# Hybrid retention and differential attention layer on one core: first transfers regrouped, first scores of four heads one slice later, last half block multiplied with normalized tokens

## The chip, the cores and the metric

The kernel runs on one core of a Trainium2 chip. The metric is the device time of one execution in microseconds (us), given as the median of several runs; a second source is one profiled execution, from which all rows below come. Engines are named as in the profile: PE (TensorE, matmuls), PEld (its weight loads, which overlap PE), DVE (VectorE), ACT (ScalarE), POOL (GpSimd) and SP (the queue that issues most transfers).

## What is computed

One encoder layer on 512 tokens of width 2048. Everything is float32 outside; inside, each matmul operand is split into a high and a low part, and a product is three matmuls.

```python
u = rmsnorm(h, attn_norm)
rq, rk, rv, rg, dq, dk, dv, dg = split(u @ w_in)
ro = retention(rope(rq), rope(rk) * RET_DK ** -0.5, rv)
ro = rmsnorm(ro, ret_gn) * silu(rg)
do = diff_attention(rmsnorm(dq, diff_qn), rmsnorm(dk, diff_kn), dv, lam)
do = rmsnorm(do, diff_subln) * (1.0 - lam_init) * silu(dg)
h = h + concatenate([ro, do]) @ w_out
gate = sigmoid(rmsnorm(h, ple_norm) @ w_ple_gate)
h = h + gate * (p @ w_ple_proj)
```

## The kernel before

Tokens lie along the free axis, features along the 128 partitions, so x is 16 tiles of 128 x 512. Each weight matrix is read once in pieces of 256 columns. `split` (L134 to L141) makes the high part on ACT (Copy, L137, or with a gain L140) and the low part on DVE (source minus high part, L138 or L141). `mm3` (L143 to L146) issues the three matmuls of a product.

**The start.** SP issues the first half of x's first tile, ACT's queue issues the first 256 columns of the dv weights and then `cols`, a small tile `ct` with all gains; SP goes on with the second half of x, the dq weights and the other tiles (L94 to L106). Six matmuls on a constant tile (`warm`) run meanwhile. The first product block needs the split of x, with its gain from `ct`, and the split of the dv weights.

**Slices.** After the start the program is a list of projections. A projection yields after each slice, twelve 512-column matmuls. `after(n, step)` puts a step into the agenda n slices ahead, and `tick` calls what is due. So attention steps stand between slices of matmuls of other projections, by tables written by hand: `QK` for the norms of q and k, `SCORES` and `TURNS` for the two heads of a pair and four blocks of 128 queries, `VALUES` for the products with v. A scheduler then orders each engine's instructions, mainly in the order in which the program writes them, and weight splits go ahead by a priority.

**Scores.** For one head and block, `scores` (L473 to L496) takes two PSUM banks from the tag `sc`, which has two. Each gets two matmuls (L484 with `k`, L485 with `kz`); DVE then writes a mask (MEMSET, L486) and takes the row maximum (TENSOR_REDUCE, L487); ACT takes the exponential out of the bank (L488) and reads the row sum. With that the bank is free. The next head's `scores` takes the same two banks. `stack_k` (L458 to L468) makes `k0`, `k1` and the low parts `kz` of a head from its normed `t_k`: two copies on ACT (L462, L463), and on DVE CAST, `kz`, CAST, `kz` (L464 to L467). There are four pairs of heads, numbered 0 to 3 here; in pairs 1 and 3 the scores stand between slices of a wide dv projection, in pairs 0 and 2 between slices of gate and q projections, where `silus` (L424 to L433) also switches ACT's function table.

**The gate stage.** After the output projection each residual tile `h_sb[b]` is split with its gain (`h_hi`, `h_lo`), unnormalized; the row factor `R1` (1/rms of each token) is multiplied in after the gate product. `output` (L834 to L842) does for one block: times R1 (DVE, L838), Sigmoid (ACT, L839), times the p projection (DVE, L840), plus h (DVE, L841), transfer out (SP, L842). The last projection has its weights in tiles of their own, and its second block of 128 features is done in two halves of 256 tokens, so that the chain behind the last matmul is short (L862 to L872).

Of the kernel before, what the change touches and what calls it, by code (L numbers as in the profile page):

```python
# [12 lines left out]
F32 = mybir.dt.float32  # L13
F32R = mybir.dt.float32r
AF = mybir.ActivationFunctionType
ALU = mybir.AluOpType
AX = mybir.AxisListType

P = 128
S = 512  # L20
D = 2048
KB = D // P
EPS = 1e-6
CW = 256
# [3 lines left out]
AHEAD = 600  # L28
WARM = 6
FIRST = ((0, 1), (1, 1)) + tuple((k, 2) for k in range(2, KB, 2))  # L30
SCORES = ((7, 11, 15, 19), (9, 13, 17, 21))
TURNS = ((10, 14, 18, 22), (12, 16, 20, 25))
VALUES = (25, 29)
QK = (4, 6)
# [4 lines left out]
def f(ap):  # L39
    return ap.bitcast(F32)  # L40
# [3 lines left out]
def tile_layer(  # L44
# [5 lines left out]
    w_out: bass.AP,  # L50
    w_gate: bass.AP,
    w_proj: bass.AP,
    cols: bass.AP,
    lams: bass.AP,
    cosT: bass.AP,
    sinT: bass.AP,
# [9 lines left out]
    nc = tc.nc  # L66
    PSUM = bass.MemoryType.PSUM

    const = ctx.enter_context(tc.tile_pool(name="const", bufs=1))
    upool = ctx.enter_context(tc.tile_pool(name="upool", bufs=1))  # L70
    wpool = ctx.enter_context(tc.tile_pool(name="wpool", bufs=4))
    vpool = ctx.enter_context(tc.tile_pool(name="vpool", bufs=1))
    onp = ctx.enter_context(tc.tile_pool(name="onp", bufs=1))
    tmp = ctx.enter_context(tc.tile_pool(name="tmp", bufs=2))
# [3 lines left out]
    def bank(tag, bufs, name):  # L78
# [5 lines left out]
    xt = [xp.tile([P, S], F32, tag=f"xt{k}", name=f"xt{k}") for k in range(KB)]  # L84
    raws = [[xp.tile([P, n, CW], F32, tag=f"raw{i}_{k}", name=f"raw{i}_{k}") for i in range(2)]
            for k, n in FIRST]
    ct = const.tile([P, 43], F32, name="ct")

    def load_w(q, b, i):
        k, n = FIRST[b]  # L90
        off = (OFF_DV, OFF_DQ)[i]
        q.dma_start(raws[b][i], w_in[k * P:(k + n) * P, off:off + CW].rearrange("(kb p) n -> p kb n", p=P))

    H = S // 2  # L94
    with tc.high_priority(offset=2 * AHEAD):
        nc.sync.dma_start(xt[0][:, :H], xT[0:P, :H])
        load_w(nc.scalar, 0, 0)
        nc.scalar.dma_start(ct, cols)
        nc.sync.dma_start(xt[0][:, H:], xT[0:P, H:])
        load_w(nc.sync, 0, 1)  # L100
        for b, (k, n) in enumerate(FIRST[1:], 1):
            for i in range(n):
                nc.sync.dma_start(xt[k + i], xT[(k + i) * P:(k + i + 1) * P, :])
                if i == 0:
                    load_w(nc.sync, b, 0)
                    load_w(nc.sync, b, 1)  # L106
# [16 lines left out]
    g_attn, g_ple, g_ret = ct[:, 0:16], ct[:, 16:32], ct[:, 32:40]  # L123
# [10 lines left out]
    def split(hi, lo, src, gain=None):  # L134

        if gain is None:
            nc.scalar.activation(hi, src, AF.Copy)  # L137
            nc.vector.tensor_tensor(lo, src, f(hi), ALU.subtract)  # L138
        else:
            nc.scalar.activation(hi, src, AF.Copy, scale=gain)  # L140
            nc.vector.scalar_tensor_tensor(lo, src, gain, f(hi), ALU.mult, ALU.subtract)  # L141

    def mm3(out, ah, al, bh, bl, start, stop):  # L143
        nc.tensor.matmul(out, lhsT=ah, rhs=bh, start=start, stop=False, skip_group_check=True)  # L144
        nc.tensor.matmul(out, lhsT=ah, rhs=bl, start=False, stop=False, skip_group_check=True)  # L145
        nc.tensor.matmul(out, lhsT=al, rhs=bh, start=False, stop=stop, skip_group_check=True)  # L146
# [62 lines left out]
    def after(n, *todo):  # L209
        agenda[clock[0] + n].extend(todo)  # L210
# [57 lines left out]
    R1 = const.tile([P, S], F32, name="R1")  # L268
# [89 lines left out]
    with start:  # L358
        ssum = xp.tile([P, S], F32, name="ssum")

        first = [[bank(*tag, f"acc_{name}0_{j}") for j in range(2)]
                 for tag, name in ((("acc", 4), "dv"), (("sc", 2), "dq"))]
        for b, (k0, n) in enumerate(FIRST):
            wh, wl = ([wpool.tile([P, 2, CW], F32R, tag=tag, name=f"{tag}{i}_{k0}") for i in range(2)]
                      for tag in ("whi", "wlo"))
            for k in range(k0, k0 + n):
                uh = upool.tile([P, S], F32R, tag=f"uh{k}", name=f"uh{k}")
                ul = upool.tile([P, S], F32R, tag=f"ul{k}", name=f"ul{k}")  # L370
                u_hi.append(uh)
                u_lo.append(ul)
                s = k - k0

                def split_w(i):
                    split(wh[i][:, s, :], wl[i][:, s, :], raws[b][i][:, s, :])

                if k == 0:
                    split_w(0)
                    split(uh[:, :H], ul[:, :H], xt[0][:, :H], g_attn[:, 0:1])  # L380
                    split(uh[:, H:], ul[:, H:], xt[0][:, H:], g_attn[:, 0:1])
                    split_w(1)
                else:
                    split(uh, ul, xt[k], g_attn[:, k:k + 1])
                    split_w(0)
                    split_w(1)
                v_products(first[0], k, wh[0][:, s, :], wl[0][:, s, :])
                fm_products(first[1], k, KB, wh[1][:, s, :], wl[1][:, s, :], u_hi, u_lo)
                sq = ssum if k == 0 else tmp.tile([P, S], F32, tag="sq", name=f"xsq{k}")
                nc.scalar.activation(sq, xt[k], AF.Square)  # L390
                if k:
                    nc.vector.tensor_tensor(ssum, ssum, sq, ALU.add)
        row_norm(ssum)

# [45 lines left out]
    with ExitStack() as st:  # L440
# [88 lines left out]
        def pair_jobs(hp):  # L529
# [26 lines left out]
            def queue_heads():  # L556
# [4 lines left out]
                for j, (s, t, v, n) in enumerate((diff_steps(2 * hp + j, pair) for j in range(2))):  # L561
                    for b in range(4):
                        after(late + SCORES[j][b], partial(s, b))
                        after(late + TURNS[j][b], partial(t, b))
# [193 lines left out]
    mixp = ctx.enter_context(tc.tile_pool(name="mixp", bufs=1))  # L758
# [20 lines left out]
    h_hi, h_lo, h_sb = [], [], []  # L779
    ssum = mixp.tile([P, S], F32, name="ssum2")  # L780
# [50 lines left out]
                fm_products(pp, k, 2, wh[:, k, :], wl[:, k, :], p_hi, p_lo)  # L831
        return pp

    def output(b, ag, pp, c):  # L834

        n = c.stop - c.start
        g = tmp.tile([P, S], F32, tag="t0", name=f"fg{b}_{c.start}")[:, :n]
        nc.vector.tensor_tensor(g, ag, R1[:, c], ALU.mult)  # L838
        nc.scalar.activation(g, g, AF.Sigmoid)  # L839
        nc.vector.tensor_tensor(g, pp[:, c], g, ALU.mult)  # L840
        nc.vector.tensor_tensor(h_sb[b][:, c], h_sb[b][:, c], g, ALU.add)  # L841
        nc.sync.dma_start(outT[b * P:(b + 1) * P, c], h_sb[b][:, c])  # L842

    def outputs(n, ag):
        pp = ple(n)
        for j in range(2):
            output(2 * n + j, ag[j], pp[j], slice(0, S))

    for n in range(7):
        run(proj_fm(w_gate, n * CW, KB, h_hi, h_lo, f"pg{n}", partial(outputs, n)))  # L850

# [2 lines left out]
    pp = ple(7, (("tp", 1), ("o", 1)))  # L854
    wv = w_gate.rearrange("(kb p) n -> p kb n", p=P)
    with tc.high_priority(offset=AHEAD):
        last = []
        for k0 in range(0, KB, 4):
            raw = wpool.tile([P, 4, CW], F32, tag="wraw", name=f"wr_pg7_{k0}", bufs=2)
            nc.sync.dma_start(raw, wv[:, k0:k0 + 4, 7 * CW:8 * CW])  # L860
            for s in range(0, 4, 2):
                wh, wl = (mixp.tile([P, 2, CW], F32R, tag=f"{t}{(k0 + s) // 2}", name=f"{t}_pg7_{k0 + s}")  # L862
                          for t in ("mh", "ml"))
                split(wh, wl, raw[:, s:s + 2, :])
                last.extend((wh[:, i, :], wl[:, i, :]) for i in range(2))
    for b, c in ((14, slice(0, S)), (15, slice(0, S // 2)), (15, slice(S // 2, S))):
        n = c.stop - c.start
        w = slice((b - 14) * P, (b - 13) * P)
        ag = bank("acc", 4, f"acc_pg7_{b}_{c.start}")[:, :n]
        for k, (wh, wl) in enumerate(last):  # L870
            mm3(ag, wh[:, w], wl[:, w], h_hi[k][:, c], h_lo[k][:, c], k == 0, k == KB - 1)
        output(b, ag, pp[b - 14], c)  # L872


def _tables():
# [49 lines left out]
```

## Time and profile before

| what | value |
|---|---|
| device time, median of 3 runs | 1083.37 us (1083.04 to 1083.54) |
| the profiled execution, device time | 1083.01 us |
| its span, first to last instruction | 1081.2 us |
| PE busy | 1074.7 us, 99% of the span |
| DVE busy | 652.9 us, 60% |
| ACT busy | 561.2 us, 52% |
| HBM read and written | 106.06 MB and 4.19 MB |

The span is 1.8 us shorter than the device time of the same execution. A busy PE is work plus pipelining: matmuls overlap, so a 512-column matmul that shows 0.39 us starts 0.23 us after the one before it, and a 256-column one with 0.28 us starts 0.12 us after.

### The profile page before, as it was taken

How to read it: one execution, taken by the hardware profiler on the slowest of the kernel's cores; microseconds unless marked ns; L12 is line 12 of the kernel's file. 1: busy time of each engine (PE TensorE's matmuls, PEld its weight loads, DVE VectorE, ACT ScalarE, POOL GpSimd, SP SyncE). 2: the span in 40 equal slices, each digit the busy share in tenths (PEclk: the TensorE clock that was granted, in tenths of full speed). 3: DMA queues.
4: the chain of work that ended last, by engine and by line, in shares of the span. 5: the costliest groups of instructions: out<-in, count | busy, mean ns of one | idle time of the engine just before them, and what ended most of it. 6: DMA issues, size and time to landing. Idle time of an engine off the chain costs nothing.

```text
span 1081.2 us, 13724 instructions
## 1 busy us (share of the span) xinstructions
PE 1074.7 (99%) x5090; PEld 900.7 (83%) x5090; DVE 652.9 (60%) x1211; ACT 561.2 (52%) x1044; POOL 4.9 (0%) x14
## 2 busy tenths in 40 slices
PE   9999999999999999999999999999999999999998
PEld 8888888888888888888888988888888888888887
DVE  8677658775968786577446866844334453334442
ACT  8477657565767755664436655743333343222330
POOL 0000000000000000000000000000000000000000
PEclk9999999999999999999999999999999999999999
DMA  9232322322232232243322332463333323333341
GB/s 318 62 95 80 96 79 79 96 81 78 79 98 72 66 98 79 79 136 92 102 87 91 97 100 75 155 200 96 97 98 98 98 88 121 124 117 114 120 136 40
DMA packets 100579, 111.15 MB, mean 103 GB/s; under 512 B 4384, under 2 KB 88992, under 8 KB 100512
## 3 DMA queue, kind: packets, MB, share of 16 engines
q1 hardware_dynamic: 97632, 105.40, 31.7%
q10 hardware_dynamic: 2880, 4.87, 1.3%
q8 instruction: 40, 0.66, 0.3%
q14 instruction: 27, 0.22, 0.1%
HBM read 106.06 MB, written 4.19 MB: 102 GB/s over the span
## 4 chain that ended last, share of the span: by engine, by line
PE 98%; DVE 1%; ACT 0%; DMA 0%; issue 0%; ACTq 0%
PE acc_pg L145 5%; PE acc_pg L144 5%; PE acc_pg L146 5%; PE acc_o L146 5%; PE acc_o L145 5%; PE acc_o L144 5%; PE acc_dv L144 3%; PE acc_dv L145 3%; PE acc_dv L146 3%; PE acc_dq L144 3%; PE acc_rg L144 3%; PE acc_dq L145 3%; PE acc_dg L144 3%; PE acc_dk L144 3%; PE acc_dg L146 3%; PE acc_dg L145 3%
## 5 line engine op out<-in xcount | busy, mean ns | idle before, releaser
L144 PE MATMUL acc_o<-mh,wh_o 128*128 128x512 f32 x256 | 99.6, 389 | 0.0
L145 PE MATMUL acc_o<-ml,wh_o 128*128 128x512 f32 x256 | 99.6, 389 | 0.0
L146 PE MATMUL acc_o<-mh,wl_o 128*128 128x512 f32 x256 | 99.6, 389 | 0.0
L137 ACT ACTIVATE wh_o<-wr_o 128x512 fp32r<-128x512 f32 x64 | 40.4, 631 | 113.4 <-PE acc_o L145 106.7
L138 DVE TENSOR_TENSOR wl_o<-wr_o,wh_o 128x512 fp32r<-128x512 f32 x64 | 44.2, 691 | 89.2 <-ACT wh_o L137 89.2
L137 ACT ACTIVATE wh_pg<-wr_pg 128x512 fp32r<-128x512 f32 x56 | 35.4, 632 | 102.1 <-PE acc_pg L145 88.5
L144 PE MATMUL acc_pg<-hh,wh_pg 128*128 128x512 f32 x224 | 87.1, 389 | 0.0
L145 PE MATMUL acc_pg<-hl,wh_pg 128*128 128x512 f32 x224 | 87.1, 389 | 0.0
L146 PE MATMUL acc_pg<-hh,wl_pg 128*128 128x512 f32 x224 | 87.1, 389 | 0.0
L138 DVE TENSOR_TENSOR wl_pg<-wr_pg,wh_pg 128x512 fp32r<-128x512 f32 x56 | 38.7, 690 | 69.4 <-ACT wh_pg L137 69.4
L145 PEld LDWEIGHTS acc_o<-ml,wh_o 128*128 128x128 f32 x256 | 48.1, 188 | 10.0
L144 PEld LDWEIGHTS acc_o<-mh,wh_o 128*128 128x128 f32 x256 | 48.1, 188 | 10.0
L146 PEld LDWEIGHTS acc_o<-mh,wl_o 128*128 128x128 f32 x256 | 48.1, 188 | 9.8
L144 PE MATMUL acc_dv<-wh_dv,uh 128*128 128x512 f32 x128 | 51.0, 398 | 0.0
L144 PE MATMUL acc_dg<-uh,wh_dg 128*128 128x512 f32 x128 | 50.8, 397 | 0.0
L144 PE MATMUL acc_dk<-uh,wh_dk 128*128 128x512 f32 x128 | 50.4, 394 | 0.0
L144 PE MATMUL acc_rg<-uh,wh_rg 128*128 128x512 f32 x128 | 50.4, 394 | 0.0
L145 PE MATMUL acc_dk<-ul,wh_dk 128*128 128x512 f32 x128 | 50.1, 391 | 0.0
L146 PE MATMUL acc_dg<-uh,wl_dg 128*128 128x512 f32 x128 | 50.1, 391 | 0.0
L146 PE MATMUL acc_dv<-wh_dv,ul 128*128 128x512 f32 x128 | 50.1, 391 | 0.0
L145 PE MATMUL acc_dg<-ul,wh_dg 128*128 128x512 f32 x128 | 50.0, 391 | 0.0
L145 PE MATMUL acc_dv<-wl_dv,uh 128*128 128x512 f32 x128 | 50.0, 391 | 0.0
(318 smaller groups left out, 2824.1 us busy)
## 6 DMA issues: line engine op xcount, KB each, us to landing
wr_o<-w_out SPq DMA_DIRECT2D x32, 512.0 KB, 3.4
wr_pg<-w_gate SPq DMA_DIRECT2D x32, 512.0 KB, 3.5
wr_dk<-w_in SPq DMA_DIRECT2D x16, 512.0 KB, 3.6
wr_dg<-w_in SPq DMA_DIRECT2D x16, 512.0 KB, 3.7
wr_rg<-w_in SPq DMA_DIRECT2D x16, 512.0 KB, 3.6
wr_dq<-w_in SPq DMA_DIRECT2D x12, 512.0 KB, 3.7
wr_rv<-w_in SPq DMA_DIRECT2D x12, 512.0 KB, 3.9
wr_dv<-w_in SPq DMA_DIRECT2D x8, 512.0 KB, 3.9
```

Of the source, the lines that this page charges most:

```text
L137: nc.scalar.activation(hi, src, AF.Copy)
L138: nc.vector.tensor_tensor(lo, src, f(hi), ALU.subtract)
L144: nc.tensor.matmul(out, lhsT=ah, rhs=bh, start=start, stop=False, skip_group_check=True)
L145: nc.tensor.matmul(out, lhsT=ah, rhs=bl, start=False, stop=False, skip_group_check=True)
L146: nc.tensor.matmul(out, lhsT=al, rhs=bh, start=False, stop=stop, skip_group_check=True)
```

## The change

Three places. At the start, the first half of x's first tile and the columns come in one transfer, from one array that the host has put together (`x0c`, 128 x 299); the dq weights go from SP's queue to ACT's; the split of x stands ahead of that of the dv weights; the first Square is done in halves. In `SCORES`, the first entry of a pair's first head goes from slice 7 to slice 8; its second head stays at slice 9. In the gate stage, the second half of the tokens of all 16 tiles is multiplied with gain and R1 and split again (`normalize`, from slice 10 of the stage on), and the last half block multiplies these; its `output` leaves out the multiplication by R1. `output` now adds into its own tile `g` and sends that, so that `h_sb` stays as it was.

```diff
-SCORES = ((7, 11, 15, 19), (9, 13, 17, 21))
+SCORES = ((8, 11, 15, 19), (9, 13, 17, 21))
...
-    ct = const.tile([P, 43], F32, name="ct")
+
+    H = S // 2
+    xc = const.tile([P, H + 43], F32, name="xc")
+    ct = xc[:, H:]
...
     with tc.high_priority(offset=2 * AHEAD):
-        nc.sync.dma_start(xt[0][:, :H], xT[0:P, :H])
+        nc.sync.dma_start(xc, x0c)
         load_w(nc.scalar, 0, 0)
-        nc.scalar.dma_start(ct, cols)
+        load_w(nc.scalar, 0, 1)
         nc.sync.dma_start(xt[0][:, H:], xT[0:P, H:])
-        load_w(nc.sync, 0, 1)
...
                 if k == 0:
+                    split(uh[:, :H], ul[:, :H], xc[:, :H], g_attn[:, 0:1])
                     split_w(0)
-                    split(uh[:, :H], ul[:, :H], xt[0][:, :H], g_attn[:, 0:1])
                     split(uh[:, H:], ul[:, H:], xt[0][:, H:], g_attn[:, 0:1])
                     split_w(1)
...
-                sq = ssum if k == 0 else tmp.tile([P, S], F32, tag="sq", name=f"xsq{k}")
-                nc.scalar.activation(sq, xt[k], AF.Square)
-                if k:
+                if k == 0:
+                    nc.scalar.activation(ssum[:, :H], xc[:, :H], AF.Square)
+                    nc.scalar.activation(ssum[:, H:], xt[0][:, H:], AF.Square)
+                else:
+                    sq = tmp.tile([P, S], F32, tag="sq", name=f"xsq{k}")
+                    nc.scalar.activation(sq, xt[k], AF.Square)
                     nc.vector.tensor_tensor(ssum, ssum, sq, ALU.add)
...
-    def output(b, ag, pp, c):
+    def output(b, ag, pp, c, scaled=False):
...
-        nc.vector.tensor_tensor(g, ag, R1[:, c], ALU.mult)
-        nc.scalar.activation(g, g, AF.Sigmoid)
+        if not scaled:
+            nc.vector.tensor_tensor(g, ag, R1[:, c], ALU.mult)
+        nc.scalar.activation(g, ag if scaled else g, AF.Sigmoid)
         nc.vector.tensor_tensor(g, pp[:, c], g, ALU.mult)
-        nc.vector.tensor_tensor(h_sb[b][:, c], h_sb[b][:, c], g, ALU.add)
-        nc.sync.dma_start(outT[b * P:(b + 1) * P, c], h_sb[b][:, c])
+        nc.vector.tensor_tensor(g, h_sb[b][:, c], g, ALU.add)
+        nc.sync.dma_start(outT[b * P:(b + 1) * P, c], g)
+
+
+    late, n_hi, n_lo = slice(S // 2, S), [], []
+    for m, v, n in (("mh", "vh", n_hi), ("ml", "vl", n_lo)):
+        for b in range(10, KB):
+            two = mixp.tile([P, 2, CW], F32R, tag=f"{m}{b}", name=f"n{m}{b}")
+            n.extend(two[:, i, :] for i in range(2))
+        four = vpool.tile([P, 4, CW], F32R, tag=v, name=f"n{v}", bufs=1)
+        n.extend(four[:, i, :] for i in range(4))
+
+    def normalize(k):
+        t = tmp.tile([P, S], F32, tag="sq", name=f"hn{k}")[:, late]
+        nc.vector.scalar_tensor_tensor(t, h_sb[k][:, late], g_ple[:, k:k + 1], R1[:, late], ALU.mult, ALU.mult)
+        split(n_hi[k], n_lo[k], t)
...
+    for k in range(KB):
+        after(10 + 2 * k, partial(normalize, k))
     for n in range(7):
         run(proj_fm(w_gate, n * CW, KB, h_hi, h_lo, f"pg{n}", partial(outputs, n)))
...
-            mm3(ag, wh[:, w], wl[:, w], h_hi[k][:, c], h_lo[k][:, c], k == 0, k == KB - 1)
-        output(b, ag, pp[b - 14], c)
+            mh, ml = (n_hi[k], n_lo[k]) if c == late else (h_hi[k][:, c], h_lo[k][:, c])
+            mm3(ag, wh[:, w], wl[:, w], mh, ml, k == 0, k == KB - 1)
+        output(b, ag, pp[b - 14], c, c == late)
```

What the scheduler makes of it, at two places. First ACT at the start of the program, before:

```order
L92 DMA raw_0_98<-w_in 128x256
L98 DMA ct<-cols 128x43
L114 ACT_TABLE_LOAD
L137 ACTIVATE whi_0_189<-raw_0_98 128x256
L140 ACTIVATE uh_193<-xt_82,ct 128x256 x2
L137 ACTIVATE whi_0_190<-raw_0_99 128x256
L390 ACTIVATE ssum<-xt_82 128x512
L140 ACTIVATE uh_226<-xt_83,ct 128x512
```

and with the change (the line numbers of the same code are one to five higher in it):

```order
L95 DMA raw_0_98<-w_in 128x256
L95 DMA raw_0_99<-w_in 128x256
L115 ACT_TABLE_LOAD
L141 ACTIVATE uh_192<-xc 128x256
L138 ACTIVATE whi_0_188<-raw_0_98 128x256
L141 ACTIVATE uh_192<-xt_82,xc 128x256
L138 ACTIVATE whi_0_189<-raw_0_99 128x256
L391 ACTIVATE ssum<-xc 128x256
L392 ACTIVATE ssum<-xt_82 128x256
L141 ACTIVATE uh_226<-xt_83,xc 128x512
```

The weights of dq have taken the place of the columns in ACT's queue, and the first split of x stands ahead of the weights' split.

Second, DVE around the first scores of pair 3 (`sc_0_0` and `sc_0_1` are the banks of the pair's first head, `t_k_1`, `k_3788`, `k_3789`, `kz_761` and `kz_762` belong to its second head, `wl_dv_11` is a weight split), before:

```order
L355 SCALAR_TENSOR_TENSOR t_k_1_3573<-sq_k_1_3737,t_k_1_3573 128x512
L486 MEMSET sc_0_0_3818 64x64
L486 MEMSET sc_0_1_3824 64x64
L487 TENSOR_REDUCE sts_0_3815<-sc_0_0_3818 128x1
L487 TENSOR_REDUCE sts_0_3815<-sc_0_1_3824 128x1
L464 CAST k_3788<-k_3788 64x512
L466 SCALAR_TENSOR_TENSOR kz_761<-t_k_1_3573,ct,k_3788 64x512
L465 CAST k_3789<-k_3789 64x512
L467 SCALAR_TENSOR_TENSOR kz_762<-t_k_1_3573,ct,k_3789 64x512
L138 TENSOR_TENSOR wl_dv_11_3963<-wr_dv_10_3923,wh_dv_11_3962 128x512
L491 RECIPROCAL rs_0_3830<-sts_0_3815 128x2
```

and with the change:

```order
L356 SCALAR_TENSOR_TENSOR t_k_1_3573<-sq_k_1_3737,t_k_1_3573 128x512
L468 CAST k_3788<-k_3788 64x512
L470 SCALAR_TENSOR_TENSOR kz_761<-t_k_1_3573,xc,k_3788 64x512
L469 CAST k_3789<-k_3789 64x512
L139 TENSOR_TENSOR wl_dv_11_3963<-wr_dv_10_3923,wh_dv_11_3962 128x512
L471 SCALAR_TENSOR_TENSOR kz_762<-t_k_1_3573,xc,k_3789 64x512
L490 MEMSET sc_0_0_3834 64x64
L490 MEMSET sc_0_1_3840 64x64
L491 TENSOR_REDUCE sts_0_3831<-sc_0_0_3834 128x1
L491 TENSOR_REDUCE sts_0_3831<-sc_0_1_3840 128x1
L139 TENSOR_TENSOR wl_dv_12_3988<-wr_dv_12_3984,wh_dv_12_3987 128x512
```

Masks and maxima of the first head have moved behind the whole `stack_k` of the second head and a weight split. PE at the same place, with the change, where the second head's scores (`sc_0_0_3884`, `sc_0_1_3890`) take the banks of the first:

```order
L348 MATMUL ss_d_3870<-sqh_d_3730,ones 128x512
L145 MATMUL acc_dv_0_3611<-wh_dv_9_3901,uh_474 128x512
L488 MATMUL sc_0_0_3884<-k_3788,qa_3531 128x128
L489 MATMUL sc_0_0_3884<-kz_761,qa_3531 128x128
L146 MATMUL acc_dv_0_3611<-wl_dv_9_3902,uh_474 128x512
L147 MATMUL acc_dv_0_3611<-wh_dv_9_3901,ul_475 128x512
L488 MATMUL sc_0_1_3890<-k_3789,qb_3532 128x128
L489 MATMUL sc_0_1_3890<-kz_762,qb_3532 128x128
L145 MATMUL acc_dv_1_3612<-wh_dv_9_3901,uh_474 128x512
```

Three dv matmuls have come ahead of or between the second head's four score matmuls, which stood together before.

## Rows read from the trace of the kernel before

**Rows 1.** Page, part 1: busy us (share of the span) and instructions.

```profile
PE 1074.7 (99%) x5090; PEld 900.7 (83%) x5090; DVE 652.9 (60%) x1211; ACT 561.2 (52%) x1044; POOL 4.9 (0%) x14
```

**Rows 2.** Chain of work that ended last, both ends: start us, us, what.

```profile
0.74 0.41 ACTq L92
...
1.18 2.96 DMA ct<-cols
...
1076.66 0.43 DVE fg L838
...
1077.12 0.42 ACT fg L839
```

**Rows 3.** Waits of PEld: what waited, us in total, times, longest us.

```profile
PEld sc L485 <- DVE kz L467: 0.4, 2, 0.2
```

**Rows 4.** Timeline of PE at scores of pairs 1, 2, 2, 3: start us, us.

```profile
199.97 0.27 PE L484 MATMUL sc<-k,qb 128*128 128x128 f32 x1
...
301.36 0.27 PE L484 MATMUL sc<-k,qb 128*128 128x128 f32 x1
...
307.38 0.39 PE L484 MATMUL sc<-k,qa 128*128 128x256 f32 x1
...
384.19 0.33 PE L484 MATMUL sc<-k,qb 128*128 128x128 f32 x1
```

**Rows 5.** Timeline of DVE at the same places, pairs 1, 2 and 3.

```profile
199.14 0.75 DVE L467 SCALAR_TENSOR_TENSOR kz<-t_k,ct,k 64x512 fp32r<-64x512 f32 x1
...
299.24 0.75 DVE L467 SCALAR_TENSOR_TENSOR kz<-t_k,ct,k 64x512 fp32r<-64x512 f32 x1
300.03 0.49 DVE L487 TENSOR_REDUCE sts<-sc 128x1 f32<-128x128 f32 x2
300.55 0.69 DVE L138 TENSOR_TENSOR wl_dq<-wr_dq,wh_dq 128x512 fp32r<-128x512 f32 x1
...
381.29 0.18 DVE L486 MEMSET sc<- 64x64 f32 x2
381.43 0.49 DVE L487 TENSOR_REDUCE sts<-sc 128x1 f32<-128x128 f32 x2
...
383.76 0.75 DVE L467 SCALAR_TENSOR_TENSOR kz<-t_k,ct,k 64x512 fp32r<-64x512 f32 x1
```

**Rows 6.** Timeline of ACT at the same places, pairs 2 and 3.

```profile
300.96 0.20 ACT L488 ACTIVATION_READ_ACCUMULATOR p<-sc,sts 128x1 f32 x1
...
383.17 0.62 ACT L137 ACTIVATE wh_dv<-wr_dv 128x512 fp32r<-128x512 f32 x1
```

**Rows 7.** Timeline of the start; in brackets idle before and what ended it.

```profile
1.46 2.93 PE L111 MATMUL warm<-wide 128*128 128x512 f32 x6 [1.46 <-DVE wide L108]
...
3.65 0.42 ACT L137 ACTIVATE whi<-raw 128x256 fp32r<-128x256 f32 x1 [0.70 <-DMA raw<-w_in]
...
4.22 0.91 ACT L140 ACTIVATE uh<-xt,ct 128x256 fp32r<-128x256 f32 x2 [0.16 <-DMA ct<-cols]
...
4.78 0.58 PE L144 MATMUL acc_dv<-whi,uh 128*128 128x256 f32 x1 [0.40 <-ACT uh L140]
...
5.77 0.28 PE L144 MATMUL acc_dv<-whi,uh 128*128 128x256 f32 x1
...
6.45 0.72 ACT L140 ACTIVATE uh<-xt,ct 128x512 fp32r<-128x512 f32 x1 [0.41 <-DMA xt<-xT]
...
8.35 0.19 PEld L145 LDWEIGHTS acc_dv<-wlo,uh 128*128 128x128 f32 x1 [0.27 <-DVE wlo L138]
```

**Rows 8.** DMA issues: queue, count, KB each, median us from issue to landing.

```profile
xt<-xT SPq DMA_DIRECT2D x2, 128.0 KB, 2.7
```

**Rows 9.** Windows: length, busy us (instructions) by engine, granted clock, DMA share, GB/s.

```profile
5.70:8.30 2.60, 2.60 (x17) 2.15 (x16) 1.38 (x4) 2.19 (x6) 0.00 (x0) 1.00 0.98 329
886.00:1054.00 168.00, 168.00 (x743) 139.16 (x742) 71.15 (x109) 51.03 (x83) 0.00 (x0) 1.00 0.38 119
1076.70:1080.80 4.10, 0.00 (x0) 0.00 (x0) 1.24 (x3) 0.42 (x1) 0.00 (x0) 1.00 0.09 32
```

More of the change, by code (lines that the diff above doesn't have):

```diff
@@ L52, in tile_layer @@
     w_proj: bass.AP,
-    cols: bass.AP,
+    x0c: bass.AP,
     lams: bass.AP,
@@ L92, in load_w @@
         q.dma_start(raws[b][i], w_in[k * P:(k + n) * P, off:off + CW].rearrange("(kb p) n -> p kb n", p=P))
-    H = S // 2
     with tc.high_priority(offset=2 * AHEAD):
-        nc.sync.dma_start(xt[0][:, :H], xT[0:P, :H])
+        nc.sync.dma_start(xc, x0c)
         load_w(nc.scalar, 0, 0)
-        nc.scalar.dma_start(ct, cols)
+        load_w(nc.scalar, 0, 1)
         nc.sync.dma_start(xt[0][:, H:], xT[0:P, H:])
-        load_w(nc.sync, 0, 1)
         for b, (k, n) in enumerate(FIRST[1:], 1):
@@ L911 @@
         "w_gate": a["w_ple_gate"][0], "w_proj": a["w_ple_proj"][0],
-        "cols": cols, "lams": lams, "cosT": cosT, "sinT": sinT, "decay": dec,
+        "x0c": np.concatenate([a["x"][0].T[:P, :S // 2], cols], 1),
+        "lams": lams, "cosT": cosT, "sinT": sinT, "decay": dec,
     }
```

## The prediction

> **What bounds the kernel now.** I began with the busy times on the page: PE is busy for 99% of the span [rows 1], DVE and ACT for about half. So the time is PE's stream of matmuls, and only two things change it: a place where that stream stops, and what lies before its first and behind its last matmul. The chain of work that ended last says what the ends are: the columns' transfer `ct`, which was issued at 1.18 us and took 2.96 us, and behind the last matmul a multiplication, a Sigmoid and two more steps [rows 2]. Stops inside are few. Among the waits of PEld I looked for those that belong to the scores: the second `kz` of a first head came late twice, 0.4 us in all [rows 3]. The timelines of PE, DVE and ACT around the first scores [rows 4 to 6] show what each of these engines does there, and that decides this case.
>
> **The change, the scores.** The move from slice 7 to slice 8 gives the first head's `kz` one slice (12 x 0.23 = 2.7 us) more, so these 0.4 us go. But the second head stays at slice 9 and needs the same two banks, so instead of two slices there is now one between them. What must happen in it: mask, maximum and Exp of the first head. DVE and ACT work in order, and the order listed above puts masks and maxima behind the second head's whole `stack_k` and a weight split. I walk this with the durations of the rows.
>
> From the end of the second `kz` to the end of the second row sum, where no other work stands between, pair 2 shows 299.24 + 0.75 = 299.99 to 300.96 + 0.20 = 301.16 [rows 5, 6]: 1.17 us. The two masks, which stand there now, add 0.15 (381.29 to 381.43) [rows 5], and the weight split that has come ahead of them 0.69 (300.55) [rows 5].
>
> - Pair 1: the last `kz` started at 199.14 [rows 5]; it goes 0.69 later for the split ahead of it and 0.10 earlier since a mask has left, and ends at 199.14 + 0.59 + 0.75 = 200.48. The banks are free at 200.48 + 0.15 + 1.17 = 201.80. PE wants the second one at 199.97 [rows 4], plus 0.23 for a dv matmul put ahead, minus the 0.2 that it no longer lost: 200.0. It stops for 1.8 us; less 0.2 it is **+1.6**.
> - Pair 3: `kz` at 383.76 + 0.69, ended at 385.20 [rows 5]; masks to 385.35; here a weight split stands between the two Exp, now as before (0.62, at 383.17) [rows 6], of which 0.52 show since starts overlap: free at 385.35 + 1.17 + 0.52 = 387.04. PE wants it at 384.19 [rows 4] plus three matmuls, 0.69: 384.88. It stops for 2.15, less 0.2: **+1.95**.
> - Pair 2: maxima came straight behind `kz`; now a split and masks stand between, less 0.05: the banks are free at 301.16 + 0.79 = 301.95. PE wants the second at 301.36 [rows 4], so it stops for 0.6. ACT goes on in order: a table load, Silu, a table load, the second head's Exp. These move by the same 0.79, and for them PE waits already at 307.38 [rows 4]. So the loss grows to **+0.8**.
> - Pair 0 has the same pattern, with some slack at the later place: **+0.7**.
>
> Sum +5.05, with the 0.4 already taken off. No other work covers it: PE had nothing to wait for at these places but this. Bounds: 0.4 us earlier in each of the four (idle in ACT or DVE that I did not see) gives +3.4; another 0.3 each, for steps queued behind that become late in their turn, gives +6.3.
>
> **The start.** Now ACT splits the weights at 3.65, waits for `ct`, splits x at 4.22, and PE begins at 4.78 [rows 7]. With the change x and columns land together. No row shows such a transfer; the nearest are the half tile, 2.7 us [rows 8], and `ct`, 2.96 [rows 2], so with an issue at 0.74, as ACT's first [rows 2], it lands between 3.44 and 3.70. Two splits of 0.46 and 0.42 [rows 7] bring PE to 4.4 to 4.7: 0.1 to 0.35 us sooner. That is not all gain, since PE waits again at 8.35 for the second tile's weights, 0.27 us [rows 7], behind x that landed at 6.45. SP issues that one transfer sooner, and an issue took 0.41 [rows 2]; if it lands so much sooner, up to 0.4 is gained, if not, 0. The DMA engines were busy for 0.98 of that stretch [rows 9], so I am nearer to the low end: **-0.2**. The Square in two halves costs ACT some 0.2 us in a gap of 0.41 [rows 7].
>
> A rule bears on this. The Trainium skill, Trainium Kernel Development and Optimization, section Key Constraints, says that transfers from all queues share the same DMA engines, and that issuing from several queues saves issue time only. By that rule the start would be worth 0 and the whole 0.2 us more. The busy share fits it [rows 9], but no row shows a transfer issued sooner.
>
> **The gate stage.** Sixteen times, DVE multiplies and subtracts and ACT copies 128 x 256, each near 0.43 [rows 2]: 14 us on DVE, 7 on ACT. In 168 us DVE is busy for 71 and ACT for 51 [rows 9]. The order puts all sixteen between nine weight splits. In these nine slices, 24.5 us, DVE has 9 x 0.69 for splits, 6 x 0.69 for one `output` pair and 14: 24.3. It just fits, and what covers a delay is that weights are split four buffers, some 8 us, ahead. I take 0; without that cover it would be up to +2. Outputs go out of `g`, whose two buffers come round only after several us more than a transfer takes.
>
> **The end.** Behind the last matmul the multiplication of 1076.66 goes; Sigmoid at 1077.12 [rows 2] starts when that did: **-0.46**, between 0.42 and 0.5. The matmuls stay as many and as long.
>
> **The sum.** +5.05 - 0.2 - 0.46 = +4.4 us. Against the profiled execution, 1083.01, that is 1087.4; the median of the runs stands 0.36 higher, so the forecast is 1083.4 + 4.4 = **1087.8**.
>
> **Rivals.**
>
> - *The banks are free in time* (not slower). Should DVE come to the masks before the second head's `stack_k` is through, Exp would be done when PE comes, and only gains would be left: -0.4 - 0.2 - 0.46, so 1082.3. It decides at the end of the second row sum: by 200.0 in pair 1 and 384.9 in pair 3, where I have 201.8 and 387.0. For it: before, in two slices, PE found the banks free or nearly so at all four places, and nothing of the work in between has grown. Against it: the order on DVE is fixed, and the maxima were done in the time in which DVE waited for ACT's copies, which now passes unused. Chance 0.11.
> - *The clock falls in the stops.* Early matmuls of 256 columns show 0.58 and from 5.77 on 0.28, after PE had worked since 1.46 [rows 7]: 4.3 us at half pace, so 2.15 lost for each fall. Two long stops would make it 1087.8 + 4.3 = 1092.1. Against it: at the end the granted clock stays at full, its level of 2.4 GHz, for 4.1 us without a matmul [rows 9], twice my longest stop. Chance 0.03. [...]
> - *The gate stage starves PE.* If those nine slices do not fit, weight splits come late: +2 on top, 1089.8. Chance 0.04.
>
> **How the numbers follow.** The forecast has 0.82. Its own bounds are 1083.4 + 3.4 - 0.4 - 0.5 = 1085.9 and 1083.4 + 6.3 - 0 - 0.42 = 1089.3; the range 1085.9 to 1089.3 leaves out the first two rivals and a little of the forecast and of the third. A measurement of this kernel tells changes of over 0.2%, 2.2 us, from none. The forecast, the clock and the gate stage lie above, 0.89; a wrong size of the stops may bring it under 2.2 in 0.03, so slower is 0.86. Within are 0.12: most of the first rival, and that. To be faster by 2.2 us the gains would have to be twice what I see: 0.02.
>
> **What the profile after would show.** Right: a wait of PEld for ACT's Exp (`p`) at the first scores of the second heads, four times, near 1.8 and 2.2 us in the two wide pairs and 0.3 to 0.6 in the others; the `kz` wait gone; PE's first product near 4.6; Sigmoid straight behind the last matmul; some 5 us of PE idle more. Wrong: no such waits and a span near 1080 us, or matmuls of 512 columns longer than 0.39 behind the stops, or waits for `wl_pg` in the gate stage.

## The result, and the profile after

The changed kernel takes 1090.26 us (median of 6 runs, 1087.77 to 1090.66), the kernel before in the same comparison 1083.16. The ratio on record is 1.0053, with a 95% interval of 1.0042 to 1.0064 (the two medians alone divide to 1.0066). So it is slower, as forecast, but 2.5 us above the forecast of 1087.8 and 1.0 above the upper end of the range. The six runs fall in two groups: two of 1087.77 and 1088.03 with a mean granted clock of 1.000, and four of 1090.22 to 1090.66 with 0.996 to 0.998. The first group is the forecast. The second has something more, which the profiled execution (1090.31 us, span 1088.5, clock 0.996) shows. The slowest run, 1090.66, has 0.998, which is a smaller loss of clock than the 0.996 of the profiled one; no trace of it was kept, and what makes it as slow as the others stays open.

The page of the changed kernel, part 1, against [rows 1]:

```profile
PE 1078.9 (99%) x5090; PEld 902.3 (83%) x5090; DVE 664.3 (61%) x1242; ACT 566.6 (52%) x1061; POOL 4.9 (0%) x14
```

PE has as many matmuls as before and is 4.2 us longer busy, so some matmuls were longer or overlapped less; the rest of the 7.3 us by which the span grew is idle. DVE and ACT did 11.4 and 5.4 us more, where the forecast had 14 and 7. The waits of PEld, and below them one line of the same view before:

```profile
PEld sc L488 <- ACT p L492: 6.6, 7, 2.3
...
PEld acc_dv L145 <- ACT whi L138: 1.0, 1, 1.0
```

```profile
PEld sc L484 <- ACT p L488: 0.4, 1, 0.4
```

The wait for `kz` of [rows 3] is gone; in its place the scores (L488) wait seven times for ACT's Exp (`p`), 2.3 us the longest, where before there was one such wait of 0.4. Four were forecast; pairs 0 and 2 wait at two places each, and pair 3 has a short one of 0.2 behind its long one. Pair 1, the timeline of PE in the changed kernel (start, us; in brackets idle before and what ended it):

```profile
199.87 0.39 PE L145 MATMUL acc_dv<-wh_dv,uh 128*128 128x512 f32 x1
201.83 0.33 PE L488 MATMUL sc<-k,qa 128*128 128x128 f32 x1 [1.58 <-ACT p L492]
...
202.97 0.41 PE L145 MATMUL acc_dv<-wh_dv,uh 128*128 128x512 f32 x1
203.20 0.60 PE L146 MATMUL acc_dv<-wl_dv,uh 128*128 128x512 f32 x1
203.60 0.63 PE L147 MATMUL acc_dv<-wh_dv,ul 128*128 128x512 f32 x1
204.03 0.63 PE L145 MATMUL acc_dv<-wh_dv,uh 128*128 128x512 f32 x1
```

Two losses can be read here. The score matmul starts 1.96 us after the one before it, where 0.23 is normal: a stop of 1.73. Then, from 203.20 on, the 512-column matmuls last 0.6 instead of 0.39 and start 0.43 apart instead of 0.23. DVE and, below it, ACT at that place:

```profile
199.31 0.69 DVE L139 TENSOR_TENSOR wl_dv<-wr_dv,wh_dv 128x512 fp32r<-128x512 f32 x1
200.02 0.75 DVE L471 SCALAR_TENSOR_TENSOR kz<-t_k,xc,k 64x512 fp32r<-64x512 f32 x1
200.78 0.19 DVE L490 MEMSET sc<- 64x64 f32 x2
201.00 0.49 DVE L491 TENSOR_REDUCE sts<-sc 128x1 f32<-128x128 f32 x2
```

```profile
201.32 0.37 ACT L492 ACTIVATE p<-sc,sts 128x128 f32<-128x128 f32 x1 [2.27 <-DVE sts L491]
...
201.93 0.20 ACT L492 ACTIVATION_READ_ACCUMULATOR p<-sc,sts 128x1 f32 x1
```

The weight split and the second `kz` come first, then masks and maxima, and ACT, idle for 2.27 us, ends the second row sum at 202.13. The walk had put the masks at 200.48 and the end at 201.80; in this execution all is about 0.3 later, because PE itself is there 0.3 later. In pair 3 the score matmul starts 2.31 us after the one before it:

```profile
388.34 0.39 PE L145 MATMUL acc_dv<-wh_dv,uh 128*128 128x512 f32 x1
390.65 0.33 PE L488 MATMUL sc<-k,qa 128*128 128x128 f32 x1 [1.92 <-ACT p L492]
```

What the granted clock did (length, busy time of PE, PEld, DVE, ACT and POOL, granted clock, DMA share, GB/s):

```profile
203.20:206.60 3.40, 3.40 (x10) 2.51 (x9) 1.71 (x8) 1.30 (x5) 0.00 (x0) 0.50 0.50 148
206.60:210.00 3.40, 3.40 (x19) 2.90 (x18) 0.93 (x3) 1.12 (x3) 0.00 (x0) 1.00 0.02 7
390.95:394.36 3.41, 3.41 (x11) 2.74 (x10) 2.86 (x10) 3.13 (x11) 0.00 (x0) 0.50 0.24 83
890.00:1062.00 172.00, 172.00 (x760) 142.13 (x759) 85.23 (x144) 58.06 (x103) 0.00 (x0) 1.00 0.37 119
```

Behind the stop of pair 1, and behind that of pair 3, the granted clock is 0.50, its level of 1.2 GHz, and in the first of these windows there are 10 matmuls where the next one, of the same length, has 19, five short ones of scores and a transpose among them. Nowhere else in the stream does it fall. The last row is the gate stage: with the 16 normalizations DVE is busy for 85 us and ACT for 58, and PE for all of the 172 us.

The two ends, ACT's and PE's timelines of the changed kernel, against [rows 7] and the end of [rows 2]:

```profile
3.77 0.51 ACT L141 ACTIVATE uh<-xc 128x256 fp32r<-128x256 f32 x1 [0.83 <-DMA xc<-x0c]
...
5.81 0.71 ACT L141 ACTIVATE uh<-xt,xc 128x512 fp32r<-128x512 f32 x1
...
1084.56 0.38 ACT L844 ACTIVATE fg<-acc_pg 128x256 f32<-128x256 f32 x1 [4.88 <-PE acc_pg L147]
```

```profile
4.64 0.87 PE L145 MATMUL acc_dv<-whi,uh 128*128 128x256 f32 x2 [0.25 <-ACT whi L138]
```

PE begins at 4.64 instead of 4.78, the second tile's split comes at 5.81 instead of 6.45, and Sigmoid waits for the last matmul alone.

Where the 7.3 us lie is found by taking the start of the same matmul, counted from the first, in both traces:

| place | later than before, us | of it stop | of it clock |
|---|---|---|---|
| start | -0.41 | | |
| pair 0 | +0.74 | 0.74 | |
| pair 1 | +3.29 | 1.7 | 1.6 |
| pair 2 | +0.78 | 0.78 | |
| pair 3 | +3.43 | 2.0 | 1.4 |
| rest, with the gate stage | +0.07 | | |
| from the last matmul's start to the end (4.89 to 4.27) | -0.6 | | |

The clock's part of pair 1 is 8 matmuls with 0.2 us more between starts each; that of pair 3 is added up in the same way.

### The profile page after: what moved, and what is told of

Same layout as the page of the kernel before. It is cut to its first block, busy times and chain, and to the rows that moved or that the text cites. A ratio compares the mean times of both kernels' runs of the same rounds, so it can differ in the third digit from the quotient of the medians.

```text
span 1088.5 us, 13793 instructions
## 1 busy us (share of the span) xinstructions
PE 1078.9 (99%) x5090; PEld 902.3 (83%) x5090; DVE 664.3 (61%) x1242; ACT 566.6 (52%) x1061; POOL 4.9 (0%) x14
## 4 chain that ended last, share of the span: by engine, by line
PE 93%; DVE 4%; ACT 2%; issue 1%; DMA 0%; DVEq 0%; ACTq 0%
PE acc_pg L145 5%; PE acc_pg L147 5%; PE acc_pg L146 5%; PE acc_o L146 5%; PE acc_o L145 5%; PE acc_o L147 5%; PE acc_rg L145 3%; PE acc_dk L145 3%; PE acc_dk L146 3%; PE acc_dk L147 3%; PE acc_rg L147 3%; PE acc_rg L146 3%; PE acc_dv L146 3%; PE acc_dv L145 3%; PE acc_dv L147 3%; PE acc_dq L145 3%
## 5 line engine op out<-in xcount | busy, mean ns | idle before, releaser
L492 ACT ACTIVATE p<-sc,sts 128x128 f32<-128x128 f32 (+3 forms) x64 | 33.3, 523 | 36.5 <-DVE sts L491 36.4
```

The costliest lines, as they stand in the source:

```text
L492: nc.scalar.activation(pt[i][:, :L], sc, AF.Exp, bias=sts[:, i:i + 1], accum_out=sts[:, 2 + i:3 + i])
```

## Experiments

**The scores back.** First which part costs what: the changed kernel without its later scores.

```diff
-SCORES = ((8, 11, 15, 19), (9, 13, 17, 21))
+SCORES = ((7, 11, 15, 19), (9, 13, 17, 21))
```

> The changed kernel with the first heads' first scores back at slice 7; start, normalized last half block and its output as changed. Theory (the scores are the whole loss; start worth 0.4, end 0.5, gate stage nothing): 1083.2 - 0.4 - 0.5 = 1082.3 us, granted clock 1.00 throughout, no wait of PEld or PE for ACT's Exp, the late kz back twice with 0.4 us in all. Rival (start or normalization cost something that the stops covered): 1083.2 or more, with a wait that the kernel before does not have.

Measured 1082.66 us (11 runs), ratio 0.9994 (0.9985 to 1.0002), mean granted clock 0.999 to 1.000 in every run. The whole loss is in one number of a table; what is left of the change gains about 0.5, which the interval doesn't tell from none.

**The scores alone.** The kernel before with only that number.

```diff
-SCORES = ((7, 11, 15, 19), (9, 13, 17, 21))
+SCORES = ((8, 11, 15, 19), (9, 13, 17, 21))
```

> The kernel before with nothing but the first scores at slice 8. Theory (the loss needs only this, stops and a fall of the clock behind the long ones): as a whole 1083.2 + 5.1 = 1088.3 us where the clock stays at 1.00 and about 1091.2 where it falls behind the stops of pairs 1 and 3, 1.5 us each. Rival (the stops come of the changed start or of DVE's additional work together with the later slice): less than 3 us above the kernel before.

Measured 1091.32 us, ratio 1.0069 (1.0057 to 1.0082): one run of 1088.63 at a mean clock of 0.999 and four of 1091.20 to 1091.64 at 0.996 to 0.998. Both numbers of the theory are met, 1088.3 and 1091.2, though here too one of the slow ones, 1091.20, has 0.998. Neither the new start nor DVE's additional work has a part in it.

**Two slices again.** The other scores and the turns follow the first head by one slice.

```diff
-SCORES = ((8, 11, 15, 19), (9, 13, 17, 21))
-TURNS = ((10, 14, 18, 22), (12, 16, 20, 25))
+SCORES = ((8, 12, 16, 20), (10, 14, 18, 22))
+TURNS = ((11, 15, 19, 23), (13, 17, 21, 26))
```

> The changed kernel with the other scores and turns a slice later as well, so that two slices lie between the first and the second head's scores again. Theory (one slice between two uses of the two banks is too short, two are enough): no wait for ACT's Exp, no late kz, clock 1.00, 1083.2 - 0.4 - 0.4 - 0.5 = 1081.9 us. Rival (the later slice itself is the harm, whatever the distance): stops remain at the first scores and the time stays above 1086. Second rival (the later turns push the products with v against the pair's end): no stop at the scores, but new waits at the turns and no gain against the kernel before.

Measured 1083.38 us, ratio 1.0002 (0.9993 to 1.0011). The four stops are gone, but the time is 1.5 us above the 1081.9 expected. Up to pair 3 PE gains 0.7 us on the kernel before, its start apart. In pair 3, which has one slice more than the others by a rule of its own (`late`), 1.5 us are lost, 1.4 of them in one stop: PE wants the banks for the first head's second block, and the second head's first block still holds one. PE and DVE there:

```profile
393.53 0.39 PE L488 MATMUL sc<-k,qb 128*128 128x256 f32 x1 [1.25 <-ACT p L492]
```

```profile
390.51 0.28 DVE L491 TENSOR_REDUCE sts<-sc 128x1 f32<-128x128 f32 x1
390.71 0.68 DVE L356 SCALAR_TENSOR_TENSOR ot<-sq_d,ot 128x512 f32<-128x512 f32 x1
...
391.43 0.75 DVE L529 SCALAR_TENSOR_TENSOR ond<-ot,g_sub,ond 128x512 f32<-128x512 f32 x1
392.10 0.68 DVE L139 TENSOR_TENSOR wl_dv<-wr_dv,wh_dv 128x512 fp32r<-128x512 f32 x1
392.70 0.28 DVE L491 TENSOR_REDUCE sts<-sc 128x1 f32<-128x128 f32 x1
```

Between the maxima of that block's two banks DVE now does the norm of another head (`ot`, `ond`) and a weight split, 2.2 us from one to the next, where elsewhere they stand together in 0.49. It is the same mechanism at another block: a maximum stands behind work that DVE could do later, and PE waits for the bank.

**Pair 3 back.** The same without pair 3's own slice, so that pair 3 runs as before.

```diff
-                late = 1 if hp == 3 else 0
+                late = 0
```

> The third experiment (all scores and turns a slice later) with pair 3 without its own additional slice, so that pair 3 runs by the same slices as in the kernel before. There the third experiment's trace gained 0.8 us up to pair 3 against its own start and lost 2.0 us in it. Theory (that loss is pair 3's wait at its second block, 1.5 us, and what goes with it): 1083.4 - 2.0 = 1081.4 us, at most a late kz of 0.2 us in pair 3. Rival (the loss is of the later slices in general): above 1083.

Measured 1081.71 us (11 runs, 1081.12 to 1082.22), ratio 0.9985 (0.9976 to 0.9994). The theory holds. The gain is 0.3 less than expected, because the expectation took pair 3's loss as 2.0 us and, counted between places where both kernels have done the same matmuls, it is 1.5. This version beats both kernels: at the scores no wait for Exp is left, and one of 0.2 us for `kz`.

**Maxima first.** Is it the distance or DVE's order? Slices as changed, but masks, maxima and Exp of the first head's first block have priority.

```diff
+                    with tc.high_priority(offset=AHEAD) if (b, j) == (0, 0) else ExitStack():
-                    nc.vector.memset(sc[A0, L - 64:L], NEG)
+                        nc.vector.memset(sc[A0, L - 64:L], NEG)
...
```

> The changed kernel with masks, maxima and Exp of the first head's first block given priority, so that on DVE they stand ahead of most of the second head's k work again; slices as changed. Theory (the order on DVE is what makes one slice too short): of the four stops, 1.6, 1.9, 0.5 and 0.7 us, at most 0.5 is left at any place, the clock stays at 1.00, and the time is 1082.3 to 1083.5 us. Rival (the distance is too short in any order): the waits for Exp stay within 0.5 us of the changed kernel's and the time above 1086. Between the two, the second head's k work comes later in turn, and PEld waits for its k or kz instead, up to 2 us in a wide pair.

Measured 1086.09 us (8 runs, 1085.73 to 1086.75), ratio 1.0026 (1.0016 to 1.0036), with a mean clock of 1.000 in every run. The waits of PEld there:

```profile
PEld sc L488 <- ACT p L493: 2.7, 6, 0.6
...
PEld sc L489 <- DVE kz L471: 1.1, 2, 0.5
PEld sc L488 <- ACT wh_dv L138: 1.0, 2, 0.5
```

It came out between the theories. The long stop of pair 1 is now two of 0.56 and 0.58 us (in pair 3 it is much the same), one that ends with ACT, with the weight split behind the Exp, and one for `kz`, which the maxima have pushed back. So DVE's order was a part of it, some 1.8 us against the changed kernel's runs at full clock; the rest, by these waits, is that one slice is not enough for `stack_k` and for the maxima together. And with no stop over 0.6 us by itself the clock never fell.

**Other banks.** The second head's first block takes two other banks.

```diff
-                    sc = bank("sc", 2, f"sc{h}_{b}_{i}")[:, :L]
+                    sc = bank(*((("tp", 1), ("o", 1))[i] if (b, j) == (0, 1) else ("sc", 2)), f"sc{h}_{b}_{i}")[:, :L]
```

> The changed kernel with the second head's first block in two other PSUM banks (of the tags tp and o) instead of the first head's two. Theory (PE stops because the first head's Exp has not yet freed the banks): the wait of PEld for ACT's Exp at the second heads' first scores goes, and the time is 1082.3 to 1083.5 us with the clock at 1.00. Rival (the second head's own k or kz, or ACT and DVE altogether, are late): PE stops there as long, now for other names, and the time stays above 1086. In between: the other banks are taken too, by the transposes and the products with v, and PE waits for those.

Measured 1092.15 us (5 runs), ratio 1.0076 (1.0064 to 1.0089): slower still. The waits of PE, and PE's timeline in pairs 1 and 3:

```profile
PE tr L509 <- ACT p L492: 6.1, 3, 2.1
```

```profile
201.28 0.22 PE L488 MATMUL sc<-k,qa 128*128 128x128 f32 x1
...
202.25 0.33 PE L489 MATMUL sc<-kz,qb 128*128 128x128 f32 x1 [0.53 <-DVE kz L471]
...
395.17 0.33 PE L509 MATMUL tr<-ident,p 128*128 128x128 f32 x1 [2.14 <-ACT p L492]
```

At the scores no wait for Exp is left; in pair 1 a late `kz` of 0.53 us is all. So the banks were what held PE, which the theory said. But the bank of the transposes (`tp`) is now held until the second head's Exp, and the first head's transposes (L509) wait for it, 2.1 us each in three of the four pairs. There is no free bank to be had at this place: what was expected as the case in between came. In this trace the clock fell behind one of these three stops (2.0, 2.2 and 2.3 us over the normal distance of two matmuls), the one of 2.2, and not behind the other two.

**The short stops alone, one long stop alone.** Pairs 0 and 2 at slice 8 and the others at 7; then pair 1 alone at slice 8.

```diff
-                        after(late + SCORES[j][b], partial(s, b))
+                        after(late + SCORES[j][b] - (hp % 2 and (j, b) == (0, 0)), partial(s, b))
```

> The changed kernel with the first scores of pairs 1 and 3 back at slice 7; pairs 0 and 2 stay at slice 8. Theory (the clock falls only behind the long stops, and the short ones cost their length): the stops of pairs 0 and 2, 0.7 and 0.8 us, on top of the first experiment's 1082.66, so 1084.2 us, granted clock 1.00 in every run. Rival (any stop at the scores can bring the clock down): runs with a clock under 0.999 and a time above 1085.5.

```diff
-                        after(late + SCORES[j][b], partial(s, b))
+                        after(late + SCORES[j][b] - (hp != 1 and (j, b) == (0, 0)), partial(s, b))
```

> The changed kernel with the first scores a slice later in pair 1 alone, the other three pairs back at slice 7. Theory (each long stop brings the clock down by itself): on top of the first experiment's 1082.66 the stop of 1.7 us, less 0.2 for the kz that is no longer late, so 1084.2 us where the clock stays at 1.00 and 1085.8 where it falls, most runs near the latter. Rival (the fall needs all four stops): every run near 1084.2.

Pairs 0 and 2: 1084.08 us, ratio 1.0010 (1.0001 to 1.0019), so 1.4 us above the first experiment where 1.5 was expected. Of its 11 runs one, of 1086.09, is above the rival's 1085.5 and one, of 1085.31, close below it, but with mean clocks of 0.999 and 1.000, no lower than in runs of 1083.6; what made them longer stays open. Pair 1: seven runs of 1083.87 to 1084.53 at 0.999 to 1.000 and four of 1085.16 to 1085.93 at 0.998. The theory's two numbers, 1084.2 and 1085.8, are there, but "most runs near the latter" is not: by these clocks one and the same stop, of 1.74 us in the profiled run, brought the clock down in 4 runs of 11.

**Pauses of chosen lengths.** Twelve pauses between 512-column matmuls in the kernel before, far from any scores.

```diff
+PAUSES = {f"{t}{i}": n for t in ("o", "pg") for i, n in enumerate((2, 4, 5, 6, 8, 12), 1)}
...
+    def pause(n, acc, name):
+        d = small.tile([P, P], F32R, tag="pz", name=f"pzd_{name}", bufs=1)
+        with tc.high_priority(offset=2 * AHEAD):
+            nc.vector.tensor_scalar(d, acc[1][:, :P], 0.0, None, ALU.mult)
+            for _ in range(n - 1):
+                nc.vector.tensor_scalar(d, f(d), 0.0, None, ALU.mult)
+        for a in acc:
+            nc.tensor.matmul(a[:, :P], lhsT=ones, rhs=d, start=False, stop=False, skip_group_check=True)
...
```

> The kernel before, without the change, with twelve pauses put between 512-column matmuls: in the middle of the six projections 1 to 6 of the output stage and again of the gate stage, DVE reads the running sum, multiplies a 128x128 tile by zero in place 2, 4, 5, 6, 8 and 12 times, and PE adds the zeros before it goes on. By DVE rows of this size, 0.28 to 0.35 us, and 0.3 to 0.5 us on the way to DVE and back, the pauses should be some 1.0, 1.6, 1.9, 2.2, 2.8 and 4.0 us, 27 us in all: 1110 us. Theory (a pause of the length that the changed kernel's wide pairs have brings the clock to its lower level for some 8 matmuls, 1.6 us each time; a pause of at most about 1.2 does not): the lower level behind the pauses of 1.6 us and more, in most cases, and never behind the shortest. Rival (the fall needs something else that the scores have, such as the short matmuls around them): no fall behind any pause. Second rival, of the prediction (idle time leaves the clock alone up to 4.1 us): none below 4.

Measured 1121.36 us (4 runs). The pauses are by the trace 0.81, 1.80, 2.07, 2.33, 2.85 and 3.90 us over the normal distance of two matmuls, each length twice within 0.01, and 27.5 us in all, as planned; the 11 us over the expected 1110 are four falls of the clock (6.4), 24 matmuls more (2.6) and 2 that I don't assign. The stretches behind both pauses of 2.07, both of 2.85, both of 3.90, one of 1.80 and one of 2.33 us, in this order (length, busy time of PE, PEld, DVE, ACT and POOL, granted clock, DMA share, GB/s):

```profile
788.00:791.40 3.40, 3.40 (x10) 2.63 (x9) 0.00 (x0) 0.00 (x0) 0.00 (x0) 0.50 0.27 95
991.50:994.90 3.40, 3.40 (x17) 2.81 (x16) 0.63 (x1) 0.63 (x1) 0.00 (x0) 1.00 0.32 112
839.20:842.60 3.40, 3.40 (x9) 2.66 (x8) 0.00 (x0) 0.17 (x1) 0.00 (x0) 0.50 0.01 2
1046.00:1049.40 3.40, 3.40 (x17) 2.79 (x16) 0.29 (x1) 0.63 (x1) 0.00 (x0) 1.00 0.19 65
866.55:869.90 3.35, 3.35 (x9) 2.57 (x9) 0.00 (x0) 0.00 (x0) 0.00 (x0) 0.50 0.00 0
1074.75:1078.10 3.35, 3.35 (x10) 2.58 (x9) 0.00 (x0) 0.00 (x0) 0.00 (x0) 0.50 0.00 0
763.50:766.90 3.40, 3.40 (x16) 2.81 (x16) 0.46 (x1) 0.63 (x1) 0.00 (x0) 1.00 0.46 154
813.50:816.90 3.40, 3.40 (x16) 2.79 (x16) 0.19 (x1) 0.63 (x1) 0.00 (x0) 1.00 0.39 132
```

Behind the first pause of 2.07 us the clock fell, behind the second it didn't; the same for 2.85; behind both of 3.90 it fell; behind 1.80 and 2.33 it stayed, the second time too, and behind both of 0.81. So no scores are needed, which ends the first rival, and idle time below 4 us is enough, which ends the prediction's. But the theory that length alone decides falls too: equal pauses between equal matmuls did both. What decides between them was not tried.

**The start alone, the end alone.** The kernel before with one end of the change each, of which the characteristic lines are:

```diff
-        nc.sync.dma_start(xt[0][:, :H], xT[0:P, :H])
+        nc.sync.dma_start(xc, x0c)
...
-        nc.scalar.dma_start(ct, cols)
+        load_w(nc.scalar, 0, 1)
...
```

> The kernel before with the changed start alone. Theory (the first tile's transfer decides the start; PE's first product 0.1 to 0.35 us sooner): 0.2 to 0.4 us below the kernel before. Rival (transfers share the same engines, so that only issue time is saved): within 0.1 us of it. The executions so far place the n-th matmul behind the start at -0.47 to +0.25 us against the profiled kernel before, so the median of several runs decides, not one trace.

```diff
+    for k in range(KB):
+        after(10 + 2 * k, partial(normalize, k))
...
+        output(b, ag, pp[b - 14], c, c == late)
```

> The kernel before with the normalized last half block and its output alone. Theory (the multiplication behind the last matmul is saved, the sixteen normalizations are hidden): 0.4 to 0.5 us from the last matmul's start to the end less, so 1082.7 us, no new wait of PE or PEld in the gate stage. Rival (the normalizations delay weight splits): waits for the gate's weights and 1083.2 or more.

The start: 1082.83 us (11 runs) against 1083.15, ratio 0.9998 (0.9989 to 1.0006). The end: 1082.68 against 1083.18, ratio 0.9994 (0.9985 to 1.0003). Both medians are where the theories put them, and neither interval excludes no change. The traces are sharper for the end: from the last matmul's start to the end of the span the end alone takes 4.34 us instead of 4.89, and no wait of PE in the gate stage has come. For the start one trace says little. The place of one and the same matmul in the stream behind the start differs by up to 0.70 us between the nine executions profiled with the new start (-0.47 to +0.23 us against the trace of before), and by 0.36 between the four with the old one (0 to +0.36). The mean of the nine is 0.34 earlier than the mean of the four, which is less than that spread. A reason for the spread stands in the end-alone trace, which has the old start:

```profile
6.69 0.41 PE L146 MATMUL acc_dv<-whi,ul 128*128 128x256 f32 x1
6.90 0.34 PE L144 MATMUL acc_dv<-whi,uh 128*128 128x256 f32 x1
7.08 0.28 PE L145 MATMUL acc_dv<-wlo,uh 128*128 128x256 f32 x1
```

Here the matmuls become short at about 7.0 us; in the trace of before the first short one is at 5.77 [rows 7], in the changed kernel at 5.35. When the clock rises differs from execution to execution, and the stream moves with it: of the nine, the two with the latest first short matmul, 6.70 and 6.93, have the latest places, +0.23 and +0.20.

## Why the prediction was right, and where it was wrong

**The scores** were right in place, mechanism and size: stops of 0.74, 1.7, 0.78 and 2.0 us where 0.7, 1.6, 0.8 and 1.95 were forecast, 5.2 in all instead of 5.05, for ACT's Exp, with the `kz` wait gone. Only the count of the waits was off, seven instead of four. The order on DVE and the durations of the trace of before were enough to walk them. The two runs at full clock, 1087.77 and 1088.03, are the forecast. *The banks are free in time* did not come.

**The clock** is the step that failed. The rival *the clock falls in the stops* was named, with two falls and a price of 2.15 us each, and was given 0.03; it came in 4 of 6 runs and is the median. The price was 1.2 to 1.6 instead of 2.15 (1.6 and 1.4 in the profiled run, half of 2.4 between the two groups of runs), so with it the rival's time would have been 1090.2 to 1091.0. What failed is the argument against it, that the clock stays at full for 4.1 us without a matmul at the end [rows 9]. It was one sample of one execution, with no matmul behind it that could have shown a loss. And the window of [rows 9] ends at 1080.80, just before the fall in the same trace:

```profile
1080.90:1081.20 0.30, 0.00 (x0) 0.00 (x0) 0.00 (x0) 0.00 (x0) 0.00 (x0) 0.50 0.00 0
```

In other executions the clock falls earlier in that same idle end; the windows of the changed kernel and of the best version (pair 3 back) there:

```profile
1084.60:1087.20 2.60, 0.00 (x0) 0.00 (x0) 0.85 (x2) 0.34 (x1) 0.00 (x0) 1.00 0.15 50
1087.30:1088.50 1.20, 0.00 (x0) 0.00 (x0) 0.00 (x0) 0.00 (x0) 0.00 (x0) 0.50 0.00 0
```

```profile
1075.95:1078.15 2.20, 0.00 (x0) 0.00 (x0) 0.85 (x2) 0.38 (x1) 0.00 (x0) 1.00 0.01 2
1078.20:1079.90 1.70, 0.00 (x0) 0.00 (x0) 0.00 (x0) 0.00 (x0) 0.00 (x0) 0.50 0.20 69
```

It is at 0.50 from 2.8 and 2.3 us after the last matmul on. In the thirteen traces of this case the fall comes between 1.9 us (the end alone) and 5.2 us (the first experiment) after the end of the last matmul, so the 4.1 us bounded nothing. In PE's stream the fall can also show late: in pair 1 of the changed kernel PE had been at work again for 1.4 us, since 201.83, when the matmuls became long. The Trainium skill, TensorE: Matmul & The Clock Gate, section Why this matters for your kernels, warns of idle gaps between matmuls, but of longer ones than these. Here the measurement decides: the clock fell behind stops of 1.7 us and more, in some executions and not in others.

**The start** was forecast at -0.2 with bounds of 0 and -0.4. The profiled execution has -0.41, but part of that is a clock that rose earlier by chance; the medians of the start alone have -0.3, which lies between the bounds. Whether the rule of the Trainium skill (Trainium Kernel Development and Optimization, Key Constraints), by which moving a transfer to another queue would be worth only its issue time, holds here is not settled by it: x's second tile was split 0.64 us sooner in the changed kernel's trace, more than the 0.41 of an issue [rows 2], but 0.3 us of a whole run is inside the interval. The prediction read the rule as a gain of 0, though by its words the 0.41 us of an issue could still be gained.

**The gate stage** cost nothing, as forecast, though the sum had come out tight (24.3 of 24.5 us): PE is busy throughout in both traces with normalizations. **The end** gave 0.5 to 0.6 instead of 0.46.

## What to carry to other kernels

Where two steps share a buffer, moving the first one later is a change of their distance, not of the first alone: walk the holder's whole release chain, engine by engine in the new order, against the point at which the next user wants it. A wait of PE has two prices, its length and, if it is long, a clock at half speed behind it: put the second price on a new stop of 1.7 us or more, the shortest behind which the clock fell here, with a chance like the 4 of 11 or 4 of 6 runs seen here rather than 0.03. Between 0.8 us, behind which it never fell, and 1.7 there is only one stop, of 1.4 us, behind which it didn't fall in the one trace taken. And an idle stretch in one trace is one draw of the clock's behaviour, not a bound.

## What the runs showed of the hardware

Three things I had not expected. The granted clock fell to its level of 1.2 GHz behind single stops of PE between 1.7 and 4 us in some cases and not in others of the same length: of two pauses of 2.07 us one, of two of 2.85 one, of two of 3.90 both, of two each of 1.80 and 2.33 none, of three stops of 2.0 to 2.3 us in one trace one, and behind one and the same stop of 1.74 us in 4 runs of 11. The stop of 1.4 us in the third experiment's trace left it at 1.00. A fall cost 1.2 to 1.6 us, behind stops of 1.7 us and pauses of 3.9 us alike, and in the idle end it came anywhere from 1.9 to 5.2 us after the last matmul. And the moment at which the clock first rises in the start differs between executions (the first short matmul stands between 5.33 and 7.08 us in the thirteen traces), which moves the whole stream by some tenths of a us and limits what one trace can say of a change at the start.
